# Two expert layers in a two-block transformer: gather operands split in two and stored by column, weight ring turned, first-norm modulation moved

## The chip, the cores and the metric

The kernel runs on one core of a Trainium2 chip. A time is the device time of one execution in microseconds (us). The kernel before took 1819.6, 1820.46 and 1828.07 us in three runs, median 1820.46 us. PE is TensorE, DVE is VectorE, ACT is ScalarE, POOL is GpSimd, and SP is the engine whose queue issues the transfers spoken of here. 1 MB below is 1,048,576 bytes, the size of one weight chunk.

## The reference, cut to what matters

There are 256 tokens of width 1024. The first block has two layers: layer 0 with a convolution and attention mixer, layer 1 with a recurrent one, each followed by a mixture of experts. All values are 32-bit floats.

```python
for layer in range(2):
    mod = silu(c) @ mod_w[layer] + mod_b[layer]
    sh1, sc1, g1, sh2, sc2, g2 = split(mod, 6)
    h = rms_norm(x, mix_norm_g[layer]) * (1 + sc1) + sh1
    mix = even_mixer(h, ...) if layer == 0 else odd_mixer(h, ...)
    x = x + g1 * mix
    h = rms_norm(x, ffn_norm_g[layer]) * (1 + sc2) + sh2
    x = x + g2 * moe(h, ...)          # 16 experts, 2 per token

# in moe, for every expert e with its tokens tok and gates g
xb = h2[tok]                                         # gather
y = (silu(xb @ w1[e]) * (xb @ w3[e])) @ w2[e]        # w1, w3: 1024 x 512, w2: 512 x 1024
out[tok] += y * g
```

The second block has two layers of feed-forward, attention with a gating unit, and feed-forward. The change does not touch it.

## The kernel before, in words

**Experts.** In an expert layer all 16 experts are computed, sorted by how many tokens they have. Seven groups stand in `GROUPS`: the first holds two experts with up to 64 rows each, the others fewer rows and more experts. For each group the weights come in as chunks of 1 MB, four for w1, four for w3, four for w2 (the last group twice as many): 96 chunks a layer. A *unit* is one group (the first) or two; `unit_of` gathers the tokens of a unit: a 0/1 matrix `oh` picks token rows on TensorE. Then per group: `up` with w1 (L1095), `Silu` (L1156), `up` with w3, the product `hm` (L1255), `turn` (four transposes, L1101), `down` with w2 (L1114), gates and `combine` (L1131, L1132), which adds to x. Of a group `down` is done while the next group is in `up`. The weight chunks are the stationary or moving operands without any conversion.

**Gather.** `xn` holds the normalised tokens, 32-bit, [token, tile, 1024]. The gather (L1038) reads a column block of `xn` as stationary operand with every fourth column (`512 * (k // 4) + k % 4 : ... : 4`) and `oh` as 32-bit moving operand. Each such matmul stands as two records in the trace. DVE and ACT copy its result out (L1049, L1052).

**Weights and queue.** SP issues the chunk transfers in program order, and each waits until its buffer's last reader is done. There are ten buffers `raw` of 1 MB in the expert phase, and four pairs `rawwH`/`rawwL` of 0.5 MB each, which share their memory tags with the split weights `wH`/`wL` of the mixers. `chunks` takes the ten and then the four in turn (`turns["all"]`); `load` takes only `raw`. At the start of an expert layer some buffers are still held by the mixer's out projection (the pairs) or by `mod_rows` (four `raw`). A further wait on SP is the load of the order of the experts (`idsi`, L1145), from which the addresses of all chunks after the first expert group's come.

**Split.** `loadw` and `split` (L301, L303) make two rounded parts H and L of a 32-bit weight: ACT writes H = round(w), DVE or POOL writes L = w - H. The mixers' projections are then three passes, H*H, L*H and H*L (L558 to L560).

**Modulation.** `mod_rows(layer, part, row)` makes one part of `mod` along the free axis: 4 MB of `mod_w`, 64 records of L365, an addition on DVE (L402), a broadcast by eight records of L407, two ACT copies (L409). `mod_cols` makes parts along partitions. Both are put into the mixers as `fills`, work for TensorE while it would wait; `FILL1` sets how many go to which place in layer 1.

**Order.** The program is written as a list of operations, and a scheduler then sets the order on each engine. An `If` on a flag (L1198, L1199) ends the expert layer: an overflow path for experts with more rows than their group allows, which is not taken here. Before it stands `ahead_of`, in which the first loads of the next stage are issued; no instruction moves across the `If`.

**Between layers.** Behind the `If` come the norm of x (square sums L448, L450; power -0.5 on POOL L335; `xn` L463, L464), transposes (L475), features `f` (L481, L483), `hH`/`hL` (L605, L606), and the projection of the odd mixer (L558 on).

## Time and profile before

| | us |
|---|---|
| median of three runs | 1820.46 |
| the profiled execution | 1823.28 |
| its span in the trace | 1821.1 |
| mixer of layer 0, to its last matmul | 0 to 201 |
| experts of layer 0 | 201 to 465 |
| norm, features, mixer of layer 1 | 465 to 582 |
| experts of layer 1 | 582 to 836 |
| second block | 842 to 1821 |

The profiled execution took 2.2 us more than its span. Engine shares over the whole span say little here, since the second block takes over half of it and has its own limit. The stages named in the table have to be looked at one by one: for each, whether TensorE waits, or the transfers do, and who releases them.

### The profile page before, as it was taken

Reading aid. Unit: us, or ns where it says so; the run is one execution under the profiler, and the core shown is the slowest. Engines: PE = TensorE matmul, PEld = TensorE weight load, DVE = VectorE, ACT = ScalarE, POOL = GpSimd, SP = SyncE. Lnnn points to the kernel's source line nnn. Section 1 sums busy time; section 2 is a strip of 40 time slices with the busy share of each in tenths; the row PEclk is TensorE's granted clock in tenths of the full one; section 3 lists DMA queues with packets and bytes.
Section 4 is the critical chain, followed back from the end, with each engine's and each line's share of the span. In section 5 each row is a group of like instructions: output and inputs, shape, how many; then the busy total and the mean of one; then the engine's idle time right before and its main releaser. Section 6 shows DMA issues by size and latency. Waiting matters only on the chain.

```text
span 1821.1 us, 23880 instructions
## 1 busy us (share of the span) xinstructions
PE 1735.9 (95%) x9320; PEld 1226.5 (67%) x9320; DVE 901.9 (50%) x1570; ACT 710.2 (39%) x1100; POOL 96.2 (5%) x138
## 2 busy tenths in 40 slices
PE   6899999998798999988999999999999999999998
PEld 4765744432675544335888888888888888888886
DVE  3893533112657522124555564655465546655554
ACT  2434311100464211004444556544354446664443
POOL 0580000000100000000000000000000000000000
PEclk9999999999899999998999999999999999999999
DMA  9947689999986899999655653555555555426530
GB/s 363 347 165 270 240 333 395 373 407 416 348 292 246 311 371 415 418 417 351 226 186 174 198 178 101 185 185 185 185 182 185 182 184 191 158 93 208 184 118 23
DMA packets 148651, 454.80 MB, mean 250 GB/s; under 512 B 8608, under 2 KB 18992, under 8 KB 130608
## 3 DMA queue, kind: packets, MB, share of 16 engines
q1 hardware_dynamic: 148528, 453.16, 67.6%
q8 instruction: 77, 1.26, 0.3%
q14 instruction: 46, 0.38, 0.1%
HBM read 452.07 MB, written 1.05 MB: 249 GB/s over the span
## 4 chain that ended last, share of the span: by engine, by line
PE 52%; ACT 0%; issue 0%; DVE 0%; POOL 0%; DVEq 0%; POOLq 0%; ACTq 0%
PE acc L321 16%; PE acc L323 16%; PE acc L322 16%; PE tp L1281 1%; PE acc L1434 1%; PE tp L491 1%; PE acc L1344 1%; PE tp L1428 0%; PE tp L1398 0%; PE acc L1373 0%; PE acc L1338 0%; ACT t L448 0%; PE acc L1339 0%; PE acc L1340 0%; ACT wH L301 0%
## 5 line engine op out<-in xcount | busy, mean ns | idle before, releaser
L303 DVE TENSOR_TENSOR wL<-raw,wH 128x1024 fp32r<-128x1024 f32 x369 | 452.5, 1231 | 400.2 <-ACT wH L301 399.5
L301 ACT ACTIVATE wH<-raw 128x1024 fp32r<-128x1024 f32 x372 | 391.0, 1058 | 425.9 <-PE acc L323 393.4
L321 PE MATMUL acc<-wH,xTH 128*128 128x512 f32 (+1 forms) x928 | 353.2, 381 | 1.2 <-ACT xTH L494 1.1
L323 PE MATMUL acc<-wH,xTL 128*128 128x512 f32 (+1 forms) x928 | 349.0, 379 | 0.2 <-DVE xTL L495 0.2
L322 PE MATMUL acc<-wL,xTH 128*128 128x512 f32 (+1 forms) x928 | 349.2, 377 | 0.0
L323 PEld LDWEIGHTS acc<-wH,xTL 128*128 128x128 f32 x928 | 174.7, 188 | 35.0 <-DVE xTL L495 1.6
L321 PEld LDWEIGHTS acc<-wH,xTH 128*128 128x128 f32 x928 | 175.1, 189 | 33.5 <-ACT xTH L494 2.1
L322 PEld LDWEIGHTS acc<-wL,xTH 128*128 128x128 f32 x928 | 175.2, 189 | 32.8
L1095 PE MATMUL acc<-raw,xg 128*64 128x512 f32 (+1 forms) x960 | 180.4, 596 | 0.0
L322 PE MATMUL acc<-wL,tH 128*128 128x512 f32 x352 | 139.1, 395 | 0.0
L321 PE MATMUL acc<-wH,tH 128*128 128x512 f32 x352 | 138.1, 392 | 0.0
L323 PE MATMUL acc<-wH,tL 128*128 128x512 f32 x352 | 137.9, 392 | 0.0
L1095 PEld LDWEIGHTS acc<-raw,xg 128*64 128x64 f32 (+1 forms) x960 | 52.1, 123 | 100.4 <-issue 95.9
L1114 PE MATMUL acc<-raw,tf 128*32 128x512 f32 (+1 forms) x416 | 86.3, 598 | 2.9 <-DMA raw<-in_ex_w_dram 2.9
L365 PE MATMUL acc<-raw,condb 128*32 128x256 f32 x768 | 71.5, 491 | 10.6 <-DMA raw<-in_mod_w_dram 10.6
L558 PE MATMUL acc<-hH,wH 128*128 128x256 f32 x256 | 75.9, 297 | 5.7 <-ACT wH L301 5.7
L1255 DVE SCALAR_TENSOR_TENSOR hm<-acc,gg,hm 128x512 f32<-128x512 f32 x14 | 10.5, 751 | 140.6 <-PE acc L1095 96.5
L335 POOL TENSOR_TENSOR rs<-ms,mhalf 128x1 f32<-128x1 f32 x22 | 12.1, 553 | 1252.2 <-DVE ms L334 1238.1
L321 PEld LDWEIGHTS acc<-wH,tH 128*128 128x128 f32 x352 | 66.1, 188 | 14.8
L323 PEld LDWEIGHTS acc<-wH,tL 128*128 128x128 f32 x352 | 66.1, 188 | 14.0
L322 PEld LDWEIGHTS acc<-wL,tH 128*128 128x128 f32 x352 | 66.2, 188 | 13.5
L560 PE MATMUL acc<-hH,wL 128*128 128x256 f32 x256 | 74.3, 293 | 0.5 <-DVE wL L303 0.5
(366 smaller groups left out, 2201.2 us busy)
## 6 DMA issues: line engine op xcount, KB each, us to landing
raw<-in_ex_w_dram SPq DMA_DIRECT2D x140, 1024.0 KB, 11.5
raw<-in_ffn_w_gate_dram SPq DMA_DIRECT2D x44, 1024.0 KB, 5.1
raw<-in_ffn_w_up_dram SPq DMA_DIRECT2D x44, 1024.0 KB, 5.2
raw<-in_ffn_w_down_dram SPq DMA_DIRECT2D x44, 1024.0 KB, 4.9
raw<-in_mod_w_dram SPq DMA_DIRECT2D x64, 512.0 KB, 8.1
rawwH<-in_ex_w_dram SPq DMA_DIRECT2D x52, 512.0 KB, 11.5
rawwL<-in_ex_w_dram SPq DMA_DIRECT2D x52, 512.0 KB, 11.4
raw<-in_w_in_dram SPq DMA_DIRECT2D x20, 1024.0 KB, 5.1
```

The lines of the kernel that those rows point to most:

```text
L301: S.activation(H, src, AF.Copy)
L303: eng.tensor_tensor(L, src, H.bitcast(F32), op=OP.subtract)
L321: TE.matmul(o, aH, bH, start=start, stop=False)
L322: TE.matmul(o, aH, bL, start=False, stop=False)
L323: return TE.matmul(o, aL, bH, start=False, stop=stop)
L365: TE.matmul(ps[32 * i:32 * i + 32, :], condb[:, k, :], quarter(raw[:, k % 2], i), start=k == 0, stop=k == 7)
L491: TE.transpose(ps[:, j, :], src[:, j * P:(j + 1) * P], ident)
L558: TE.matmul(o, ws[kk][0][:, cs], hH[:, k, :], start=k == 0 and c % 2 == 0, stop=False)
L560: TE.matmul(o, ws[kk][1][:, cs], hH[:, k, :], start=False, stop=k == 7 and c % 2 == 1)
L1095: TE.matmul(ps[c:c + w, :], xg[:, k, c:c + w], ws[e][j], start=k == 0, stop=k == 7)
L1114: TE.matmul(y[h][c:c + w, :], tf[:, k, c:c + w], ws[e][j][:, half(h)], start=k == 0, stop=k == 3)
L1281: TE.transpose(ps[:, j, :], hm[:, j * P:(j + 1) * P], ident)
```

## The change

It has six parts. (1) `xn` is replaced by `xH` and `xL`, the two rounded parts, stored [token, tile, column block, 128], so that a column block is contiguous. ACT writes the normalised row permuted into a scratch tile (`t512`, a ring of two that `add_rows` uses as well), ACT makes `xH`, POOL makes `xL`. The gather becomes 32 single-record matmuls where it was 16 of two records. (2) The rows of w2 are taken as `p*4+j`, so that `hm` is stored [row, 4, 128]: `Silu` and the product write with a stride, the transposes read contiguous. (3) `turns["all"]` starts at 3 instead of 0: chunks 1 to 6 go to `raw`, 7 to 10 to the four pairs, then `raw` again. (4) `order_of`, which gives `idsi`, is called ahead of the first gather. (5) Before the `If` of layer 0 the 4 MB of `mod_w` for `mod_rows(1, 2)` are queued (`rows_load`), then 2 MB of `od_in`, whose first split stands ahead of the `If` still. `mod_rows(1, 2)` moves from the middle of the odd mixer to the place right behind the norm (`fills(1)`). (6) `Singly`, which only the overflow path uses, holds one 512-wide tile.

```diff
-FILL1 = (0, 1, 1)
+SOON = (6, 6)
+FILL1 = (0, 1, 0)
...
+    def rows_load(layer, part):
+        for u in range(4):
+            early[layer, part, u] = load(kp(a["mod_w"][layer])[:, 2 * u:2 * u + 2, part * D:(part + 1) * D])
...
-            self.xn = pl.tile([P, 2, D], F32, name="xn", bufs=1)
+            self.xH, self.xL = [pl.tile([P, 2, KD, P], F32R, name=n, bufs=1) for n in ("xH", "xL")]
...
-                    S.activation(self.xn[:, t, half(hh)], x[:, t, half(hh)], AF.Copy, scale=self.r[:, t:t + 1])
+                    xn, ks = small([4, P], "t512"), slice(4 * hh, 4 * hh + 4)
+                    S.activation(xn.rearrange("p k q -> p q k"), x[:, t, half(hh)].rearrange("p (q k) -> p q k", k=4),
+                                 AF.Copy, scale=self.r[:, t:t + 1])
+                    split(self.xH[:, t, ks, :], self.xL[:, t, ks, :], xn, G)
...
             hL = featL = pf.tile([P, KD, T], F32R, name="hL")
+            fills(1)
             input_features(hH, hL, nx, A, B)
...
-                            TE.matmul(ps[:, kk, :], xn[:, t, 512 * (k // 4) + k % 4:512 * (k // 4) + 512:4],
-                                      oh[:, t, :N].bitcast(F32), start=t == 0 and kk == 0, stop=t == 1 and kk == 1)
+                            for part in (xH, xL):
+                                TE.matmul(ps[:, kk, :], part[:, t, k, :], oh[:, t, :N],
+                                          start=part is xH and t == 0 and kk == 0, stop=part is xL and t == 1 and kk == 1)
...
-                    TE.transpose(pt[:, k, :], hm[:, 256 * (k // 2) + k % 2:256 * (k // 2) + 256:2], ident)
+                    TE.transpose(pt[:, k, :], hm[:, k, :], ident)
...
-                hm = px.tile([P, 512], F32, name="hm")
-                S.activation(hm, h1, AF.Silu)
+                hm = px.tile([P, 4, P], F32, name="hm")
+                S.activation(by_row(hm), rows_in(h1), AF.Silu)
...
-            turns.pop("all", None)
+            turns["all"] = sum(n for _, n in raws) - SOON[layer] - 1
             for kind in range(3):
                 for hf in range(2):
                     weights(0, kind)(hf, True)
+            first = one_hot((0,), pos)
+            order_of()
+            weights(1, 0)(0, True)
+            gates_of()
             unit_of(0)
             in_order()
-            weights(1, 0)(0, True)
...
                 def ahead_of():
 
+                    if not layer:
+                        rows_load(1, 2)
                     for hf in range(2):
-                        unit(*((first_ffn, 0) if layer else (od_in, D)), hf, False, lead=() if layer else LEAD[hf])
+                        unit(*((first_ffn, 0) if layer else (od_in, D)), hf, False if layer else "raw")
```

On SP at the start of the experts of layer 0, before (a row `raw` is a 1 MB chunk, a pair `rawwH`, `rawwL` is one chunk too; `idsi` is the order of the experts):

```order
L266 DMA raw<-in_ex_w_dram 128x2048 x10
L279 DMA rawwH<-in_ex_w_dram 128x1024
L279 DMA rawwL<-in_ex_w_dram 128x1024
L279 DMA rawwH<-in_ex_w_dram 128x1024
L279 DMA rawwL<-in_ex_w_dram 128x1024
L1145 TENSOR_LOAD idsi
```

and of the changed kernel at the same place:

```order
L267 DMA raw<-in_ex_w_dram 128x2048 x6
L280 DMA rawwH<-in_ex_w_dram 128x1024
...
L280 DMA rawwL<-in_ex_w_dram 128x1024
L267 DMA raw<-in_ex_w_dram 128x2048 x2
L1166 TENSOR_LOAD idsi
```

The dots stand for six rows, the rest of four pairs. Chunks 7 to 10 moved from `raw` to the pairs, chunks 11 and 12 from the pairs to `raw`; the wait for `idsi` stands behind chunk 12 in both.

On ACT around the `If` at the end of the experts of layer 0, before (`yp` is the last group's result, `raw_3358` and `raw_3368` the first two chunks of `od_in`, `t512` a scratch tile for the square sums):

```order
L301 ACTIVATE yp_3332<-yg_3338 128x512
L301 ACTIVATE wH_3360<-raw_3358 128x1024
L301 ACTIVATE wH_3364<-raw_3358 128x1024
L1198 TENSOR_LOAD flagi_1765
...
L448 ACTIVATE t512_4370,ss4_4368<-x_75 128x512
L301 ACTIVATE wH_3370<-raw_3368 128x1024
L301 ACTIVATE wH_3374<-raw_3368 128x1024
L448 ACTIVATE t512_4372,ss4_4368<-x_75 128x512
L448 ACTIVATE t512_4379,ss4_4368<-x_75 128x512
L464 ACTIVATE xn_4442<-x_75,rs_4369 128x512 x2
L481 ACTIVATE f_4447<-tp_4448,A11_4389 128x256
```

and of the changed kernel (`raw_3447` and `raw_3449` are the first two chunks of `od_in`, queued behind 4 MB of `mod_w`):

```order
L303 ACTIVATE yp_3413<-yg_3419 128x512
L303 ACTIVATE wH_4748<-raw_3447 128x1024
L303 ACTIVATE wH_4752<-raw_3447 128x1024
L1226 TENSOR_LOAD flagi_1778
...
L457 ACTIVATE t512_4571,ss4_4569<-x_75 128x512
L457 ACTIVATE t512_4573,ss4_4569<-x_75 128x512
L457 ACTIVATE t512_4580,ss4_4569<-x_75 128x512
L303 ACTIVATE wH_4804<-raw_3449 128x1024
L476 ACTIVATE xn_4686<-x_75,rs_4570 128x512 x2
L303 ACTIVATE wH_4808<-raw_3449 128x1024
L493 ACTIVATE f_4691<-tp_4692,A11_4590 128x256
```

The first split still stands ahead of the `If`, but its chunk is now the fifth in the queue and not the first; half of the second split stands between the `xn` and the first `f`.

On PE behind the same `If`, of the changed kernel (before, one row of 16 transposes L475 stood between the `If` and L558; L573 is what L558 was):

```order
L1227 UNCONDITIONAL_BRANCH
L367 MATMUL acc<-raw,condb 32x256 x32
L487 MATMUL tp<-cst,xn 128x128 x8
L416 MATMUL acc<-t_4640,cst 128x256 x4
L487 MATMUL tp<-cst,xn 128x128 x8
L573 MATMUL acc<-hH,wH 128x256
```

The matmuls of `mod_rows(1, 2)` (L367) and its broadcast (L416) moved here, the broadcast between the two halves of the transposes; each such matmul stands as two records in the trace.

## Rows read from the trace of the kernel before

**Rows 1.** The page, part 1: busy time, share of the span, instructions.

```profile
PE 1735.9 (95%) x9320; PEld 1226.5 (67%) x9320; DVE 901.9 (50%) x1570; ACT 710.2 (39%) x1100; POOL 96.2 (5%) x138
```

**Rows 2.** Windows, experts of layer 0: stretch, length, busy per engine, PEclk, DMA share, GB/s.

```profile
195.00:210.00 15.00, 12.88 (x96) 9.34 (x98) 8.93 (x28) 5.44 (x11) 2.05 (x20) 0.84 0.07 29
...
253.00:280.00 27.00, 27.00 (x179) 7.96 (x171) 4.02 (x6) 2.46 (x4) 0.00 (x0) 1.00 0.71 254
...
355.00:360.00 5.00, 5.00 (x20) 2.01 (x20) 0.83 (x3) 0.00 (x0) 0.00 (x0) 1.00 0.29 61
360.00:459.00 99.00, 91.77 (x442) 31.83 (x444) 19.23 (x34) 8.05 (x15) 0.00 (x0) 1.00 1.01 410
```

**Rows 3.** Windows, experts of layer 1, same columns.

```profile
643.00:660.00 17.00, 17.00 (x116) 6.39 (x116) 5.39 (x9) 1.90 (x4) 0.00 (x0) 1.00 0.86 298
660.00:831.00 171.00, 161.34 (x814) 65.53 (x809) 35.94 (x64) 17.11 (x32) 0.00 (x0) 0.99 1.02 416
```

**Rows 4.** Waits of SP's queue, 185 to 480 us: total, times, longest.

```profile
SPq L266 <- PE acc L1095: 71.6, 33, 15.5
...
SPq L266 <- PE acc L365: 20.3, 4, 18.2
```

**Rows 5.** Timeline of SP's issues: start, time, engine, line, transfer.

```profile
210.46 3.71 SPq L266 DMA_DIRECT2D raw<-in_ex_w_dram  x4
...
224.94 0.36 SPq L279 DMA_DIRECT2D rawwH<-in_ex_w_dram  x1
...
230.18 28.40 SPq L266 DMA_DIRECT2D raw<-in_ex_w_dram  x10
```

**Rows 6.** Windows, records of L1038 alone (busy PE, PEld, PEclk, DMA share, GB/s).

```profile
217.00:228.00 11.00, 8.19 (x32) 7.69 (x32) 1.00 1.02 403
241.00:251.00 10.00, 7.82 (x32) 7.54 (x32) 1.00 1.01 419
```

**Rows 7.** Groups by line on PE: busy us, mean ns of one | idle before.

```profile
L1281 PE MATMUL tp<-cst,hm 128*128 128x128 f32 x176 | 23.9, 273 | 0.0
```

**Rows 8.** Groups by line on PEld, same columns.

```profile
L1038 PEld LDWEIGHTS tp<-oh,xn 128*128 128x128 f32 x256 | 61.9, 327 | 14.5 <-issue 10.0 <-ACT xg L1049 4.4
...
L1281 PEld LDWEIGHTS tp<-cst,hm 128*128 128x128 f32 x176 | 20.4, 141 | 3.7 <-DVE tL L303 1.0
```

**Rows 9.** Timeline of PE between the layers.

```profile
473.57 2.33 PE L475 MATMUL tp<-cst,xn 128*128 128x128 f32 x8 [9.11 <-DVE xn L463]
...
477.96 0.44 PE L558 MATMUL acc<-hH,wH 128*128 128x256 f32 x1
478.24 0.28 PE L559 MATMUL acc<-hL,wH 128*128 128x256 f32 x1
478.36 0.28 PE L560 MATMUL acc<-hH,wL 128*128 128x256 f32 x1
```

**Rows 10.** Groups by line on POOL, same columns.

```profile
L699 POOL TENSOR_TENSOR cv<-cv,tap 128x256 f32<-128x256 f32 x30 | 29.2, 973 | 0.1
...
L303 POOL TENSOR_TENSOR wL<-raw,wH 128x1024 fp32r<-128x1024 f32 x3 | 7.0, 2356 | 256.1 <-ACT wH L301 256.1
```

**Rows 11.** Timeline of ACT, end of the mixer of layer 0.

```profile
198.72 1.34 ACT L457 ACTIVATE xn<-x,rs 128x512 f32<-128x512 f32 x2 [0.37 <-POOL rs L335]
```

**Rows 12.** Timeline of DVE there: the last addition to x.

```profile
202.20 1.28 DVE L502 TENSOR_TENSOR x<-x,t 128x512 f32<-128x512 f32 x2
```

**Rows 13.** Timeline of ACT between the layers.

```profile
462.42 1.99 ACT L301 ACTIVATE wH<-raw 128x1024 fp32r<-128x1024 f32 x2
466.00 0.63 ACT L448 ACTIVATE t<-x 128x512 f32<-128x512 f32 x1 [1.59 <-DVEq L1199]
```

**Rows 14.** Records of L365 in the odd mixer: count, times, first and last start.

```profile
L365 PE MATMUL acc<-raw,condb x64: 379/379/403, 501.2 to 504.5; 128*32 128x256 f32 x64
```

**Rows 15.** Timeline of PE in the odd mixer: the broadcast.

```profile
506.31 1.99 PE L407 MATMUL acc<-t,cst 128*128 128x256 f32 x8 [1.41 <-DVE t L402]
```

**Rows 16.** Timeline of PE at the end of the experts of layer 0.

```profile
457.50 0.62 PE L1114 MATMUL acc<-rawwH,tf 128*32 128x512 f32 x1 [0.67 <-DMA rawwH<-in_ex_w_dram]
```

More of the change, by code (lines that the diff above doesn't have):

```diff
@@ L283, with __init__, __getitem__ @@
     class Singly:
-        def __init__(self, ap, pl):
-            self.ap, self.pl, self.held = ap, pl, {}
-        def __getitem__(self, j):
-            if j not in self.held:
-                v = self.pl.tile([P, 1024], F32, name="one", bufs=2)[:, :self.ap.shape[2]]
-                nc.sync.dma_start(v, self.ap[:, j, :])
-                self.held[j] = v
-            return self.held[j]
+        def __init__(self, ap, pl, j=None):
+            self.ap, self.pl, self.j = ap, pl, j
+        def __getitem__(self, at):
+            if self.j is None and self.ap.shape[2] > 512:
+                return type(self)(self.ap, self.pl, at)
+            j, cols_ = (at, slice(0, 512)) if self.j is None else (self.j, at[1])
+            v = self.pl.tile([P, 512], F32, name="one", bufs=1)
+            nc.sync.dma_start(v, self.ap[:, j, cols_])
+            return v
     def after(ins):
@@ L305, with loadw @@
     turn_of = [0]
-    def loadw(ap, pool_every=0, lead=(), begin=None, then=None):
-        w = load(ap)
+    def loadw(ap, pool_every=0, lead=(), begin=None, then=None, w=None):
+        w = load(ap) if w is None else w
         n, b = ap.shape[1] // 2, ap.shape[2]
@@ L399, in mod_rows, with get @@
         w = kp(a["mod_w"][layer])[:, :, part * D:(part + 1) * D]
-        ps = mod_quarters([once(lambda u=u: load(w[:, 2 * u:2 * u + 2, :])) for u in range(4)],
+        def get(u):
+            return lambda: early.pop((layer, part, u), None) or load(w[:, 2 * u:2 * u + 2, :])
+        ps = mod_quarters([once(get(u)) for u in range(4)],
                           lambda raw, i: raw[:, 256 * i:256 * i + 256])
@@ L535, in out_proj @@
                 take(t, h)
-    ahead = {}
+    ahead, fetched = {}, {}
     def unit(wi, col, u, take=True, **kw):
-        if not take:
-            ahead[id(wi), col, u] = loadw(wi[:, 4 * u:4 * u + 4, col:col + 512], **kw)
+        key, ap = (id(wi), col, u), wi[:, 4 * u:4 * u + 4, col:col + 512]
+        if take == "raw":
+            fetched[key] = load(ap)
+        elif not take:
+            ahead[key] = loadw(ap, **kw)
         else:
-            return ahead.pop((id(wi), col, u), None) or loadw(wi[:, 4 * u:4 * u + 4, col:col + 512], **kw)
+            return ahead.pop(key, None) or loadw(ap, w=fetched.pop(key, None), **kw)
     def proj_f(wi, col, hH, hL, lead=((), ()), then=None, ps=None, halves=(0, 1)):
@@ L1004, in in_order @@
                 V.scalar_tensor_tensor(one, at(rk), 1.0, down_(slot), op0=OP.add, op1=OP.is_equal)
-                def picked(o, v):
-                    V.tensor_mul(tmp, one, at(v))
-                    V.tensor_reduce(o[:, :NS], tmp, axis=AX.X, op=OP.add)
-                    if v is not slot:
-                        V.tensor_copy(o[:, NS:], v[:, NS:16])
                 picked(ids16, slot)
@@ L1015, in in_order @@
                 V.tensor_copy(idsi[:, :16], ids16)
+            def in_order():
                 for t in range(2):
@@ L1254, in moe @@
                 hm = hm_
[L1255 removed]
+                times(hm, h3, gg)
                 if n % 2 == 0 and n < n_groups - 1:
```

43 lines of the change are left out of this document (26 added, 17 removed).

## The prediction

> **What bounds the kernel now.** I read the page first, then windows of busy time and transfer rate by stage, then the waits of SP's queue, and the timelines where one stage ends and the next begins. TensorE is busy for 95% of the span [rows 1], but that is a mean over stages with two limits. The second block, over half of the span, is not changed. In the two expert layers the transfers are the limit: from 360 to 459 us the DMA share is 1.01 at 410 GB/s while TensorE idles 7.2 us of 99, and from 660 to 831 us it is 1.02 at 416 GB/s with 9.7 us idle [rows 2, 3]. One chunk (1,048,576 bytes) at 416 GB/s is 2.52 us. TensorE's last wait for a weight in layer 0 ends at 457.50 [rows 16]; half a chunk, 1.26 us, is still to come, so the expert weights have landed at about 458.8. I call that moment X. A saving on TensorE inside an expert layer counts only as far as it moves X, that is, as far as buffers come free earlier at a place where the transfers stood still. Such places, against 416 GB/s: 195 to 210 us loses 14.0 us (29 GB/s), 253 to 280 loses 10.5 (254 GB/s), 355 to 360 loses 4.3 (61 GB/s), 360 to 459 loses 1.4 [rows 2]. In layer 1 the stretch from 643 to 660 loses 4.8 [rows 3].
>
> **Gather.** The 32 records of the first gather keep TensorE busy 8.19 us, those of a later one 7.82 [rows 6]. Each stationary load takes 327 ns, against 141 ns for one read in contiguous columns [rows 8]. The new form has 32 matmuls of one record. At 256 columns the rounded form starts every 0.12 us (478.24, 478.36) [rows 9]: 32 x 0.12 = 3.8 us. At 128 columns the nearest row has 23.9 us for 176, 0.136 us each [rows 7], so 4.3 us at most. The saving is 8.2 - 4.1 for the first unit and 7.8 - 3.8 for the three others: 16 us of TensorE per layer, 32 in all. If the rounded form were no faster than the old records (0.24 us each), the saving is zero; if all of it were on the path, 32 us. I take neither, since TensorE waits for weights at the end.
>
> **What of it moves X.** The early turn of the ring lets chunks 7 to 10 start at about 197 instead of 210.46 [rows 5], since the out projection frees the pairs sooner than `mod_rows` frees four `raw` (SP waits 18.2 us for it in one stretch) [rows 4]. That fills some 10 us of the first hole. But SP issues in order, and the pairs then hold the first half of w2 of the first group, so that the two chunks behind number 22 wait for `down` of that group, where before they waited for `up` of the next (15.5 us, the longest wait) [rows 4]. By the gathers TensorE is about 6 us earlier there, by a later start of the router (below) 2 us later, and the pair is read later in the program: chunk 24 comes within 1 us of the old time, so the early start is lost again behind it. What remains are the holes behind chunk 24: 4.2 of the 10.5 us (the rest is that wait), 4.3 at 355 to 360, which is the gather of two units holding up `up`, and 1.4: together 9.9 us. TensorE is then 6 to 10 us ahead, which closes such holes. Layer 0: -10, with ends -13 (chunk 24 a little early too) and -3 (new stalls). In layer 1 the hole is 4.8 us, of which I take off 2 us for the later router: -2.8, ends -5 and +1. At the end of the layer the last chunk is a whole `raw` instead of two halves, so TensorE starts it half a chunk later: +1.3 in layer 1; in layer 0 the next stage waits for transfers anyway.
>
> **Router.** `xL` is made by POOL. From 0.973 us at 256 elements and 2.356 at 1024 [rows 10], 512 elements are 1.43 us by interpolation. ACT begins the normalised row at 198.72 with 0.7 us for each half [rows 11]; with two `xH` of about 0.6 the POOL subtractions run to about 203.6. They hold both scratch tiles that the last additions to x need, which before ended at 203.48 [rows 12]. The last addition ends at about 205.6: +2.1 us for everything up to the first gather, in both layers. It is hidden in layer 0 and charged above in layer 1. The earlier order of the experts gives back at most 1.8 us on SP, at 224.94 [rows 5]. The strided writes of `xn` and `hm` I cost at nothing: `Silu` and the product stand beside `up`; without that cover they would cost some tenths of a microsecond per group.
>
> The rows show that a strided read costs a load 327 instead of 141 ns [rows 8]. The Trainium skill, SBUF — State Buffer, section "Door 1: The DMA port swizzle", says that accesses which go to a new 16-byte line each time pay a penalty. By that rule the new writes of the row, 512 bytes apart, would be slower; with the ratio of these loads, 2.3, four of 0.7 us become 1.6 each, and the sum would be about 3.6 us worse in layer 1. The same page's section "Who interferes with whom" has a DVE instruction with two inputs from SBUF block a POOL instruction that reads; no row here separates that from POOL's own time.
>
> **Between the layers.** The first split of `od_in` stays ahead of the `If`, but its chunk now lands behind four of `mod_w`: X + 5 x 2.52 = X + 12.6. Before, ACT ran the two halves at 462.42 to 464.41 and began the square sums at 466.00, X + 7.2 [rows 13]. Now the halves end at X + 14.6, the square sums begin at X + 16.2, and POOL's second `wL` (2.36 us) [rows 10] stands ahead of the power, which gives `xn` at X + 19.5. Then DVE has the next `wL` and the addition of `mod_rows` ahead of `f`, and the eight broadcast records (2 us) stand between the transposes. The projection starts at X + 28; before it started at 477.96 [rows 9], X + 19.2: +8.8 us. The 64 records of `mod_rows` fall in the time in which TensorE waits for `mod_w` anyway. What goes from the odd mixer is 3.66 us of L365 (501.2 to 504.9) [rows 14], 1.41 of waiting and 1.99 of broadcast [rows 15]: -7.1. Net +1.7. Ends: -6 if the scheduler's order costs nothing, +9 if the odd mixer had slack for those 7.1 us.
>
> **Sum.** -10 - 2.8 + 1.3 + 1.7 = -9.8 us. Against the profiled execution, 1823.28, that is 1813.5. That execution is 2.8 us above the median of the runs, 1820.46, to which I hold the forecast: 1810.7.
>
> **Rivals.**
> - Forecast, 42%: 1803 to 1817.
> - More comes out, 17%: chunk 24 comes 3 us earlier, all holes close, and the late start between the layers costs only what `mod_rows` saved: -13 - 5 + 1.3 - 3 = -20, 1801 us. For it: TensorE is ahead by 6 us when those chunks are wanted. Against it: the pair is the last of the group to be read.
> - Nothing, 23%: the holes move instead of closing, since SP's order and the eight chunks under way set them. Then -2.5 in layer 0 and 0 in layer 1, with +1.3 and +1.7: 1821. For it: 71.6 us of SP's waiting is on `up` [rows 4], which is not shorter.
> - Slower, 13%: ACT stands at the first split of `od_in` with four chunks ahead of it, and the odd mixer had room for `mod_rows`, so that the 8.8 us stay. This decides from the point where layer 0 gains under 5 us: -3 + 8.8 + 1.3 + 2 = +9, 1829.5. For it: the order of ACT is fixed ahead of the `If`. Against: TensorE waited only 9.11 us there and is busy behind it.
> - By the rule on lines, 5%: strided writes make ACT late in each router phase: -9.8 + 3.6 and as much for the groups' `hm`, 1818.
>
> **How the numbers follow.** Half a per cent is 9.1 us, about what a measurement tells from no change: faster is below 1811.4. The forecast lies just inside it, and of its own range the part below that bound is the larger one by the holes that could close, so of its 42% I count 28 as faster and 14 as the same; more, 17, is faster; "nothing" gives 21 to the same and 2 to slower, the rule 5 to the same, "slower" 13 to slower. That is faster 0.45, same 0.40, slower 0.15. The range 1798 to 1828 takes in the full closing of the holes at one end and most of the slow case at the other; the likeliest case by itself is 1803 to 1817.
>
> **What would show it.** Right: the gather's records fall to about 4 us per unit; SP issues chunks 7 to 10 near 197 and waits for `down` behind chunk 22; the dip at 355 to 360 is gone; the projection starts some 28 us behind X, and L367 stands ahead of the transposes; the odd mixer is 7 us shorter. Wrong: the last weight of layer 0 lands at 456 or later, or TensorE waits for rows of the gather, or the second block's time changes.

## The result, and the profile after

The change makes the kernel slower: 1834.23 us median (1832.84 to 1836.38) against 1820.13 (1819.6 to 1828.07) for the kernel before, four runs each, a ratio of 1.0068 with the interval 1.0039 to 1.0098. The forecast was 1810.7 with a range of 1798 to 1828; the time lies above it. The profiled execution has a span of 1834.6 us where the one before had 1821.1, and a mean granted clock of 0.973 where it had 0.982.

I read the two traces stage by stage, each stage from one instruction that both kernels have to the next (us from the span's start):

| where | before | after | the stage alone | predicted for it |
|---|---|---|---|---|
| first gather, layer 0 | 217.8 | 219.5 | +1.7 | +2.1 |
| last combining matmul, layer 0 | 464.1 | 462.7 | -3.1 | -12 |
| first matmul of the odd mixer's projection | 478.0 | 485.0 | +8.4 | +8.8 |
| first matmul of its recurrent gates | 527.1 | 527.5 | -6.6 | -7.1 |
| first addition to x | 575.9 | 580.2 | +3.9 | 0 |
| first gather, layer 1 | 595.5 | 604.6 | +4.8 | +2 |
| last combining matmul, layer 1 | 836.1 | 851.2 | +6.0 | -3.5 |
| last matmul | 1813.6 | 1826.5 | -2.2 | 0 |

The predicted end of layer 0's experts was -10 in all, and the 3.5 of layer 1 are the 4.8 us of its hole taken whole, less 1.3 for the last chunk. So the two moves between the layers, the largest changes in the table, were sized well, and they nearly cancel. The loss is in layer 1 and its approach, and layer 0's experts gave 3 us where 12 were expected.

The page's first part, beside [rows 1]:

```profile
PE 1724.8 (94%) x9320; PEld 1201.3 (65%) x9320; DVE 908.8 (50%) x1570; ACT 722.0 (39%) x1108; POOL 106.6 (6%) x146
```

TensorE has less to do, ACT and POOL more. Now the windows of layer 0, which answer to [rows 2] (length, busy time of PE, PEld, DVE, ACT and POOL, granted clock, DMA share, GB/s):

```profile
195.00:210.00 15.00, 10.96 (x77) 8.11 (x75) 7.51 (x20) 7.24 (x12) 4.57 (x22) 0.82 0.78 291
...
220.00:225.00 5.00, 3.79 (x24) 3.53 (x24) 4.83 (x22) 0.91 (x2) 0.00 (x0) 0.66 0.00 0
225.00:230.00 5.00, 5.00 (x18) 2.91 (x20) 5.00 (x35) 2.58 (x4) 0.00 (x0) 0.50 0.88 331
230.00:235.00 5.00, 5.00 (x20) 1.46 (x18) 4.52 (x31) 0.00 (x0) 0.00 (x0) 0.82 0.36 116
...
253.00:280.00 27.00, 26.96 (x179) 7.38 (x172) 3.79 (x5) 2.76 (x4) 0.00 (x0) 1.00 0.59 221
355.00:360.00 5.00, 5.00 (x25) 1.85 (x26) 0.93 (x6) 0.41 (x1) 0.00 (x0) 1.00 1.01 421
360.00:459.00 99.00, 86.08 (x397) 28.37 (x394) 18.72 (x27) 7.02 (x11) 0.00 (x0) 0.97 1.02 416
```

The dip at 355 us is gone (421 GB/s where there were 61), and the early start is there (291 against 29). But 220 to 225 us moves nothing at all, and the hole from 253 to 280 us, of which 4.2 us were to close, grew instead: 221 GB/s against 254. Layer 1 begins 9.1 us later than before, so its windows are counted from the first gather (604.6 and 595.5): 20 us from 30 us behind it on, then the next 20. First after, with the long stretch that answers to [rows 3] as a third line, then before:

```profile
634.60:654.60 20.00, 20.00 (x158) 6.33 (x159) 3.57 (x14) 3.21 (x6) 0.00 (x0) 1.00 0.38 137
654.60:674.60 20.00, 20.00 (x152) 9.46 (x152) 6.33 (x13) 3.24 (x5) 0.00 (x0) 1.00 0.97 380
657.00:843.00 186.00, 169.99 (x876) 61.73 (x875) 41.40 (x70) 21.06 (x35) 0.00 (x0) 0.97 1.01 415
```

```profile
625.50:645.50 20.00, 20.00 (x161) 8.25 (x161) 3.66 (x15) 3.17 (x7) 0.00 (x0) 1.00 0.71 274
645.50:665.50 20.00, 20.00 (x156) 7.23 (x156) 5.15 (x8) 2.46 (x4) 0.00 (x0) 1.00 0.89 328
```

The hole costs 20 x (274 - 137) / 416 = 6.6 us of transfer time more than before, and the next 20 us give 20 x (380 - 328) / 416 = 2.5 back. The first 5 us behind the gather lose another 4.8 (nothing moves, where before had 397 GB/s), and the 22 us ahead of the gather gain 2.1 by the early start (280 GB/s against 240). That is 6.8 us, near the 6.0 by which the stage is longer. Behind it the transfers are saturated (1.01), so nothing more comes back.

Who holds the queue is in the waits of SP, 185 to 480 us, which answer to [rows 4]:

```profile
...
SPq L267 <- PE acc L1116: 28.7, 15, 7.5
SPq L280 <- PE acc L1135: 21.1, 2, 15.1
...
SPq L1166 <- DVE pos L1018: 9.9, 1, 9.9
```

L280 issues the pairs, L1135 is `down`. Two waits of the pairs for `down` take 21.1 us, and one of them, 15.1 us, is now the longest wait. The timeline of SP's issues shows where they stand, first in layer 0, then in layer 1:

```profile
243.96 0.33 SPq L280 DMA_DIRECT2D rawwH<-in_ex_w_dram  x1
244.58 0.33 SPq L280 DMA_DIRECT2D rawwL<-in_ex_w_dram  x1
260.56 0.34 SPq L280 DMA_DIRECT2D rawwH<-in_ex_w_dram  x1
267.13 0.33 SPq L280 DMA_DIRECT2D rawwL<-in_ex_w_dram  x1
...
629.96 0.33 SPq L280 DMA_DIRECT2D rawwL<-in_ex_w_dram  x1
651.91 0.34 SPq L280 DMA_DIRECT2D rawwH<-in_ex_w_dram  x1
653.63 0.33 SPq L280 DMA_DIRECT2D rawwL<-in_ex_w_dram  x1
```

Chunk 22 goes out at 243.96 and 629.4, then the queue stands, until chunk 23 follows at 260.56 with its first half. In the kernel before the queue stands behind chunk 22 too, but for `up`, and is let go earlier. These are its chunks 23 and 24 in either layer:

```profile
257.30 1.28 SPq L266 DMA_DIRECT2D raw<-in_ex_w_dram  x2
...
635.68 0.91 SPq L266 DMA_DIRECT2D raw<-in_ex_w_dram  x2
```

Two pairs, chunks 25 and 26, go out right behind them (258.80 to 260.45 and 636.80 to 638.53), and only then does the queue stand at `down` of the first group. So that stop came four chunks earlier in the queue by the change: chunk 23 is 3 us late with its first half in layer 0 and 10 with its second, 16 and 18 in layer 1, of which 9.1 are the later start of the layer.

Why the second half comes 6.6 us behind the first in layer 0 is in the timeline of PE:

```profile
257.51 1.06 PE L1116 MATMUL acc<-raw,xg 128*32 128x512 f32 x6
258.60 1.93 PE L1135 MATMUL acc<-rawwH,tf 128*64 128x512 f32 x6
260.46 3.62 PE L1116 MATMUL acc<-raw,xg 128*32 128x512 f32 x26
264.01 0.64 PE L1135 MATMUL acc<-rawwH,tf 128*64 128x512 f32 x1
264.02 0.64 PE L1135 MATMUL acc<-rawwL,tf 128*64 128x512 f32 x1
...
266.01 1.50 PE L1135 MATMUL acc<-rawwL,tf 128*64 128x512 f32 x5
```

`down` of the first group (L1135) does not run through: it begins on `rawwH` at 258.60, `up` of the next group (L1116) stands between, and `rawwL` is read to the end only at 267.5. One wait for a pair is a wait for the whole interleaved stretch.

The gather's records by themselves, in the windows of [rows 6] (PE, PEld, granted clock, DMA share, GB/s):

```profile
217.00:228.00 11.00, 6.04 (x32) 5.51 (x32) 0.71 0.36 133
241.00:251.00 10.00, 4.26 (x32) 3.88 (x32) 1.00 1.00 409
```

At the full clock the 32 records take 4.26 us where they took 7.82, and a stationary load takes 205 to 207 ns where it took 327 [rows 8]. The first gather keeps TensorE for 6.04 us since the granted clock falls to 0.50 in that place; before it was 1.00 there.

### The profile page after: what moved, and what is told of

It is laid out like the page before. It is cut to its first block, busy times and chain, and to the rows that moved or that the text cites. A ratio compares the mean times of both kernels' runs of the same rounds, so it can differ in the third digit from the quotient of the medians.

```text
span 1834.6 us, 23902 instructions
## 1 busy us (share of the span) xinstructions
PE 1724.8 (94%) x9320; PEld 1201.3 (65%) x9320; DVE 908.8 (50%) x1570; ACT 722.0 (39%) x1108; POOL 106.6 (6%) x146
## 4 chain that ended last, share of the span: by engine, by line
PE 52%; DVE 0%; issue 0%; ACT 0%; POOL 0%; DVEq 0%; POOLq 0%; ACTq 0%
PE acc L323 16%; PE acc L325 16%; PE acc L324 16%; PE tp L1313 1%; PE acc L1466 1%; PE tp L503 1%; PE acc L1376 1%; PE tp L1460 0%; DVE wL L305 0%; PE tp L1430 0%; PE acc L1405 0%; PE acc L1370 0%; PE acc L1371 0%; PE acc L1372 0%; ACT wT L1462 0%
## 5 line engine op out<-in xcount | busy, mean ns | idle before, releaser
L1116 PE MATMUL acc<-raw,xg 128*32 128x512 f32 (+1 forms) x896 | 174.9, 633 | 11.5 <-DMA raw<-in_ex_w_dram 11.2
L1116 PEld LDWEIGHTS acc<-raw,xg 128*32 128x32 f32 (+1 forms) x896 | 46.8, 126 | 118.7 <-issue 87.6
L1135 PE MATMUL acc<-raw,tf 128*32 128x512 f32 (+1 forms) x512 | 111.3, 598 | 4.9 <-DMA raw<-in_ex_w_dram 4.9
L1185 DVE SCALAR_TENSOR_TENSOR hm<-acc,gg,hm 128x512 f32<-128x512 f32 x14 | 15.6, 1112 | 182.8 <-PE acc L1116 126.1
L303 ACT ACTIVATE yp<-yg 128x512 fp32r<-128x512 f32 x28 | 17.6, 628 | 208.8 <-DVE yg L1144 208.8
L367 PE MATMUL acc<-raw,condb 128*32 128x256 f32 x768 | 73.8, 504 | 20.1 <-ACTq L1227 9.6
L573 PE MATMUL acc<-hH,wH 128*128 128x256 f32 x256 | 76.0, 298 | 5.7 <-ACT wH L303 5.7
```

Source lines behind the costliest of these rows:

```text
L303: S.activation(H, src, AF.Copy)
L367: TE.matmul(ps[32 * i:32 * i + 32, :], condb[:, k, :], quarter(raw[:, k % 2], i), start=k == 0, stop=k == 7)
L573: TE.matmul(o, ws[kk][0][:, cs], hH[:, k, :], start=k == 0 and c % 2 == 0, stop=False)
L1116: TE.matmul(ps[c:c + w, :], xg[:, k, c:c + w], ws[e][j], start=k == 0, stop=k == 7)
L1135: TE.matmul(y[h][c:c + w, :], tf[:, k, c:c + w], ws[e][j][:, half(h)], start=k == 0, stop=k == 3)
```

## The experiments

All are changes of the kernel after, unless said. In the expectations A is the theory that the ring's new turn costs the time (A1: by what the pairs then hold), C2 that the early order of the experts does, D that the place of the column filler does, T that the place of `od_in` does. The others are told in words. The kernel before was measured again beside each set of runs, with medians of 1820.1 to 1822.1 us, so a difference of medians between two changed kernels is uncertain by one or two microseconds; the ratio to before, which stands behind each time, is the better measure.

**The ring's turn undone.**

```
-            turns["all"] = sum(n for _, n in raws) - SOON[layer] - 1
+            turns.pop("all", None)
```

> The changed kernel with one part undone: the ring of weight buffers starts at 0 again (chunks 1 to 10 raw, 11 and 12 pairs), all else as changed. Theory A (the turned ring makes the two chunks behind number 22 wait until down of the first group has read its pairs): chunks 23 and 24 are released by up again, the hole of the transfers at 253 to 270 us shrinks by 6 us, that at 640 to 655 by about 10, and the time falls by 12 to 18 us, to 1816 to 1822. Theory B (TensorE comes late out of the router and runs at half clock, whatever the ring): the time stays within 4 us of the changed kernel's 1834.

1826.25 us, 1.0021 (1.0009 to 1.0034) of before: 8 us of the 14 come back, less than expected. The experts of layer 1, from the first gather to the last combining matmul, take 238.1 us; after has 246.6 and before 240.6. In layer 0 it is 240.9 against 243.2 and 246.3. The windows of the first hole:

```profile
253.00:280.00 27.00, 26.93 (x174) 7.64 (x169) 5.45 (x18) 4.00 (x7) 0.00 (x0) 1.00 0.69 259
```

259 GB/s is close to the old 254. So the rest of the change does shorten the experts by 5.4 and 2.5 us, and the turn takes 2.3 and 8.5 of it away.

**The turn alone, put into the kernel before.**

```
-            turns.pop("all", None)
+            turns["all"] = 3
```

> The kernel before with one part added: the ring starts at 3 in both layers. Theory A (chunks 23 and 24 wait for down of the first group, which costs more than the early start of chunks 7 to 10 gives): 6 to 11 us slower than before, most of it in layer 1. Rival (the turn hurts only where the router is late): within 3 us of before.

1833.17 us, 1.0069 (1.0052 to 1.0086): the one line costs as much as the whole change. Two windows, of this kernel and then of before:

```profile
253.00:265.00 12.00, 12.00 (x80) 3.43 (x72) 0.00 (x0) 1.19 (x2) 0.00 (x0) 1.00 0.17 49
628.00:642.00 14.00, 14.00 (x124) 4.34 (x116) 0.75 (x1) 1.19 (x2) 0.00 (x0) 1.00 0.01 3
```

```profile
253.00:265.00 12.00, 12.00 (x92) 3.44 (x84) 0.00 (x0) 1.19 (x2) 0.00 (x0) 1.00 0.62 228
628.00:642.00 14.00, 14.00 (x130) 4.80 (x133) 2.36 (x13) 2.32 (x5) 0.00 (x0) 1.00 0.59 229
```

In layer 1 the transfers stand still for 14 us (3 GB/s). The experts there take 249.1 us against 240.6. In layer 0 the early start pays for the stall (246.1 against 246.3). The longest wait of a pair for `down` in layer 1 is 20.3 us; before it was 9.5. The traced execution is 7.7 us longer than the traced one of before, and layer 1's experts alone are 8.5 longer; where the rest of the 12.5 us between the medians goes, no trace shows.

**The turn kept, with other chunks in the pairs.**

```
-SOON = (6, 6)
+SOON = (4, 4)
```

> The changed kernel with SOON = (4, 4): the ring is turned further, so that chunks 5 to 8 (w3 of the first group) go to the pairs and chunks 9 to 16 to raw. The pairs are wanted again by chunks 19 to 22. Theory A1 (what costs is that the pairs hold the first half of w2, which down of the first group reads late): SP no longer waits for down ahead of chunk 23, the hole at 253 to 268 us shrinks to what the kernel before has, and the time is 1820 to 1827, as with the ring from 0 or better. Rival A2 (any turn from 0 costs, by the order of the rest of the ring): 1832 or more.

1823.41 us, 1.0013 (1.0003 to 1.0022), 10.8 us below after. The pairs now hold chunks 5 to 8, the four of w3, whose reader `up` comes one step earlier in the program than `down`. The window and the issues of this kernel:

```profile
253.00:265.00 12.00, 11.93 (x90) 3.35 (x84) 0.00 (x0) 1.51 (x2) 0.00 (x0) 1.00 0.97 382
```

```profile
247.04 0.34 SPq L280 DMA_DIRECT2D rawwL<-in_ex_w_dram  x1
253.77 21.46 SPq L267 DMA_DIRECT2D raw<-in_ex_w_dram  x10
```

The pause after the pairs is 6.4 us where it was 16, and the experts of layer 0 take 234.8 us, 11.4 less than before the change. That is about the 12 us which the forecast gave this stage, though it looked for them in the holes behind chunk 24 and counted the early start as lost; the gain needs the pairs to hold something that is read soon. In layer 1 the same turn gives 242.3, still worse than no turn (238.1): SP still waits once for `down` there, now with a `raw` (7.4 us). So what the pairs hold is about half of the turn's cost in layer 1; the rest stays with the turn itself.

**The first split of `od_in` loaded ahead of `mod_w` again**, with `mod_rows` where the change put it.

```
+    for hf in range(2):
+        unit(*((first_ffn, 0) if layer else (od_in, D)), hf, False, lead=() if layer else LEAD[hf])
     if not layer:
         rows_load(1, 2)
-    for hf in range(2):
-        unit(*((first_ffn, 0) if layer else (od_in, D)), hf, False if layer else "raw")
```

> The changed kernel with the two chunks of od_in queued and split ahead of the 4 MB of mod_w between the layers. Theory T (ACT waits at the first split of od_in for the fifth chunk in the queue, which puts the projection of layer 1 at 22 us behind the last expert matmul instead of 13.5): the projection starts 5 to 7 us earlier, and the time is 1827 to 1830. Rival: TensorE then waits for mod_w, which now lands last and stands ahead of the transposes, and the scan of the odd mixer sets its end anyway: the time is 1832 to 1836.

1828.1 us, 1.0032 (1.0015 to 1.0048): 6.1 us less than after. Timelines of ACT and of PE, after's two first and then this kernel's:

```profile
470.63 2.00 ACT L303 ACTIVATE wH<-raw 128x1024 fp32r<-128x1024 f32 x2 [9.37 <-DMA raw<-in_od_in_w_dram]
472.89 0.63 ACT L457 ACTIVATE t<-x 128x512 f32<-128x512 f32 x1 [0.26 <-ACTq L1227]
```

```profile
472.73 6.04 PE L367 MATMUL acc<-raw,condb 128*32 128x256 f32 x64 [9.60 <-ACTq L1227]
...
485.00 0.36 PE L573 MATMUL acc<-hH,wH 128*128 128x256 f32 x1
```

```profile
461.04 3.88 ACT L303 ACTIVATE wH<-raw 128x1024 fp32r<-128x1024 f32 x4
468.08 0.63 ACT L457 ACTIVATE t<-x 128x512 f32<-128x512 f32 x1 [3.15 <-DVEq L1227]
```

```profile
480.62 0.36 PE L573 MATMUL acc<-hH,wH 128*128 128x256 f32 x1
```

ACT stood 9.37 us for `od_in` behind 4 MB of `mod_w`, and TensorE waited 9.60 for ACT at the `If`. With `od_in` first the square sums (L457) start 4.8 us earlier and the projection 4.4.

**The additions to x without a scratch tile.**

```
-        V.tensor_mul(tmp, ps, row[:, half(h)])
-        V.tensor_add(x[:, t, half(h)], x[:, t, half(h)], tmp)
+        V.tensor_mul(ps, ps, row[:, half(h)])
+        V.tensor_add(x[:, t, half(h)], x[:, t, half(h)], ps)
```

> The changed kernel with the gated addition behind the mixers (add_rows) written through PSUM in place, so that it needs no scratch tile and doesn't wait for POOL's xL. Theory B1 (the shared scratch ring costs the router 2 us a layer): the last addition to x ends 2 us earlier in both layers, first gathers 2 us earlier, and the time falls by 3 to 5 us, to 1829 to 1831. Rival: another wait takes its place (the square sums use the same scratch ring): within 1.5 us of 1834.

1831.91 us, 1.0049 (1.003 to 1.0067): 2.3 us, under what was expected, and by the intervals not clear of after. The trace shows it: the first gathers come 1.7 and 3.3 us earlier. DVE in layer 0, after and then this kernel:

```profile
202.19 0.69 DVE L513 TENSOR_TENSOR t<-acc,g 128x512 f32<-128x512 f32 x1 [4.68 <-POOL xL L305]
...
204.04 1.28 DVE L514 TENSOR_TENSOR x<-x,t 128x512 f32<-128x512 f32 x2
```

```profile
201.95 1.28 DVE L513 TENSOR_TENSOR x<-x,acc 128x512 f32<-128x512 f32 x2
```

The 4.68 us wait for POOL's `xL` is the scratch tile that the prediction named; without it the last addition is back at 201.95 (before: 202.20 [rows 12]).

**The order of the experts worked out late again** (`order_of` behind `unit_of(0)`, the load of the next w1 after it).

```
-            order_of()
-            weights(1, 0)(0, True)
             gates_of()
             unit_of(0)
+            order_of()
             in_order()
+            weights(1, 0)(0, True)
```

> The changed kernel with the order of experts worked out behind the first gather again. Theory C2 (the early order puts DVE's work ahead of the copies out of the first gather, TensorE waits 1.2 us there, its clock falls to half at 222 us): no such wait, the granted clock at 220 to 230 is 0.9 or more, up of the first group ends 3 to 4 us earlier in both layers, and the time falls by 3 to 7 us, to 1827 to 1831. Rival (the rounded gather is too light by itself, or the idle time in the router decides): the clock falls all the same, chunks 13 and 14 come 1.7 us later, and the time is 1834 to 1837.

1834.62 us, 1.0073 (1.0054 to 1.0091): no difference from after. The first gather still waits 1.2 us for ACT, and the clock still falls in it. The theory that the early order is to blame fell.

**The first gather issued twice.** The 32 matmuls of the first unit run once more into the same bank.

```
+    if N == P:
+        for kk in range(2):
+            k = 2 * k2 + kk
+            for t in range(2):
+                for part in (xH, xL):
+                    TE.matmul(ps[:, kk, :], part[:, t, k, :], oh[:, t, :N], ...)
```

> The changed kernel with the first gather's matmuls of each layer issued twice into the same place (the second pass overwrites the first), so TensorE has 3.6 us more to do there. Theory C (the short gather leaves TensorE waiting for the copies out, its granted clock falls to half at 222 us and up runs at half speed until 232): the clock stays at 1.0 there, up is 3 to 5 us shorter, and the time is within 2 us of 1834 although work was added. Rival (the clock has nothing to do with it): up begins 3.6 us later in each layer and the time is 1839 to 1842.

1847.77 us, 1.0137 (1.0113 to 1.0162): 13.5 us more. More work for TensorE in that place did not keep the clock up; it only made the stretch longer, in both layers (from the first gather to the last combining matmul 250.6 us in layer 0 and 250.9 in layer 1).

**The second column filler.**

```
-FILL1 = (0, 1, 0)
+FILL1 = (0, 1, 1)
```

> The changed kernel with FILL1 = (0, 1, 1) as before: one filler of modulation columns goes back behind the first output branch of the odd mixer. Theory D (the moved filler lets the last output branch end late, so that its gelu and with it hH come late to the out projection: stalls of 3.5 and 1.6 us and a fall of the clock at 555 to 566 us): out projection of layer 1 ends 4 us earlier, time 1829 to 1831. Rival: the filler only stands elsewhere and the scan is late anyway: within 1.5 us of 1834.

1839.43 us, 1.0097 (1.0075 to 1.012): slower, against the expectation. The edit was not like for like: since `mod_rows` is already taken from the list of fillers, the second filler now comes ahead of the recurrent gates, which start 11 us later (538.4 against 527.5; 3.5 of them stand already at the projection). From there to the first addition it is 48.9 us, as before the change (48.8); after has 52.7. But the stretch holds no column filler now (7.5 us of TensorE), where both other kernels have one in it, so this run decides nothing on theory D.

**Only the gather and w2's new rows** (ring, early order, fillers and the moves between the layers undone; the edits are those above and these):

```
-FILL1 = (0, 1, 0)
+FILL1 = (0, 1, 1)
...
-            fills(1)
...
-                    if not layer:
-                        rows_load(1, 2)
```

> Of the change only the gather in two rounded parts by column block (with POOL's xL and the rows of w2 as p*4+j); the ring starts at 0, the order of experts is late, and the modulation between the layers is as before. Theory G (TensorE's saving of 32 us is worth nothing because the expert layers wait for transfers, and the router loses 2 us a layer and the clock): 1820 to 1826, no faster than before. Rival (the gather saves, and the other parts spoil it): 1808 to 1815.

1819.0 us, 0.9988 (0.9975 to 1.0001): some 2 us below before, hardly to be told from it, and in neither expected range. The experts take 240.7 and 237.0 us (before 246.3 and 240.6), 9 us less; the stretch from the first addition to the first gather of layer 1 takes back 4.9 (24.5 against 19.6).

**The same with the additions in place of the scratch tile.**

```
...
-        V.tensor_add(x[:, t, half(h)], x[:, t, half(h)], tmp)
+        V.tensor_add(x[:, t, half(h)], x[:, t, half(h)], ps)
```

> Of the change only the gather, with the gated addition in PSUM: no turned ring, order of experts late, between the layers as before. If the router's wait for POOL is what is left of the gather's cost: 2 to 4 us under the run with the gather alone, 0.3 to 0.4% under the kernel before. If the wait is replaced by another: the same as the gather alone, 0.1 to 0.2% under it.

1817.64 us, 0.9978 (0.9969 to 0.9987): faster than before, by 2 to 6 us. Against the run with the gather alone it is 1.4 us by the medians and 1.8 by the ratios, between the two expectations and not clear of noise.

**Three repairs together**: ring undone, `od_in` first, additions without scratch.

```
+            turns.pop("all", None)
...
+                    for hf in range(2):
+                        unit(..., hf, False, lead=() if layer else LEAD[hf])
...
+        V.tensor_add(x[:, t, half(h)], x[:, t, half(h)], ps)
```

> The changed kernel with three repairs: ring from 0, the gated addition in PSUM, od_in ahead of mod_w. If their effects add (ring -8 and addition -2.3 by the runs so far, od_in -5): 1818 to 1820. If the holes only move: 1823 to 1827.

1816.5 us, 0.9968 (0.9955 to 0.9981). Singly they gave 8.0, 6.1 and 2.3 us, 16.4 together; after less 16.4 is 1817.8. They add.

**The three repairs with the old gather** (`xn` in f32, read with a stride, two records each), w2's rows as in the change.

```
-                            for part in (xH, xL):
-                                TE.matmul(ps[:, kk, :], part[:, t, k, :], oh[:, t, :N], ...)
+                            TE.matmul(ps[:, kk, :], xn[:, t, 512 * (k // 4) + k % 4:512 * (k // 4) + 512:4],
+                                      oh[:, t, :N].bitcast(F32), ...)
```

> The kernel with the three repairs, but the old gather: normalised rows in 32 bits, strided columns, two records for each matmul, nothing on POOL. Theory G2 (the new gather moves the end of the expert layers by 4 to 6 us each, as the stretch from the first gather to the last combine says: 240 and 237 us where it was 246 and 241): 4 to 8 us slower than the run with three repairs. Theory C3 (the clock, which falls to half in the first gather in each run with the new one and did not before, takes it back): the granted clock at 215 to 230 stays at 1.0, and the time is within 2 us of the run with three repairs.

1819.37 us, 0.9991 (0.9981 to 1.0). Against the three repairs the medians differ by 2.9 us and the ratios by 0.0023, which is 4.2: so much is the new gather worth here, though a later unit saves 3.6 us of TensorE and the first 2.2. The two intervals touch, so the size is rough. The clock, of this kernel and then of the last kernel below, whose first gather starts within 1 us of this one's:

```profile
215.00:220.00 5.00, 4.80 (x21) 4.53 (x22) 2.76 (x14) 0.46 (x1) 0.00 (x0) 0.66 0.99 416
220.00:225.00 5.00, 5.00 (x20) 4.01 (x20) 2.96 (x12) 0.92 (x2) 0.00 (x0) 1.00 1.02 412
```

```profile
215.00:220.00 5.00, 3.54 (x24) 3.21 (x24) 4.83 (x22) 0.91 (x2) 0.00 (x0) 0.83 0.16 66
220.00:225.00 5.00, 5.00 (x18) 2.92 (x20) 5.00 (x35) 2.58 (x4) 0.00 (x0) 0.50 0.90 329
```

With the old gather TensorE is busy 4.80 of 5 us at the start of the gather, at a mean granted clock of 0.66, and is back at the full clock behind it. With the new one it is busy 3.54 of 5 at 0.83, and the next 5 us run at the half. So the clock falls in both, but for longer with the new gather: as (1 - granted clock) x length these ten microseconds lose 1.7 and 3.4 us. The other traces agree. In or right behind the first gather of layer 0 the kernel before loses nothing, the turn alone 1.7 us, and each run with the new gather 3.4 to 5.1; in layer 1 the three kernels with the old gather lose 1.7 each, those with the new one 3.4 to 5.1. Theory C3 did not come out as it stands: the clock did not stay at 1.0 here, and the time is 2.9 us over the three repairs and not within 2. But part of what the new gather saves does go back into the clock.

**The three repairs and the column fillers in the order 0, 0, 1.**

```
-FILL1 = (0, 1, 0)
+FILL1 = (0, 0, 1)
```

> The kernel with the three repairs (ring from 0, addition in PSUM, od_in first) and FILL1 = (0, 0, 1), by which the last filler of modulation columns stands behind the whole last branch of the odd mixer again and not ahead of its last eight steps. Theory D2 (those last eight steps end 8 us later, so gelu, hH and the out projection come 3 to 4 us late; from the first recurrent-gate matmul to the first addition to x it is 52.5 us where it was 48.8): that stretch falls to 49, the time is 2 to 4 us under the run with three repairs. Rival: the filler only stands elsewhere, same time within 1 us.

1815.41 us, 0.9962 (0.9948 to 0.9975). From the recurrent gates to the first addition it is 50.3 us where the three repairs have 52.5; the total can't be told from theirs. The wait that goes is in the traces: with the order 0, 1, 0 the last filler begins 15.8 us behind the first gate matmul, ahead of the end of the output branch, and the out projection then waits for ACT's `hH` (3.48 us in after, 3.47 in the three repairs). Here and in the kernel before it begins 18.6 us behind it, and that wait is gone.

**The turn with SOON = (4, 4), `od_in` first, additions without scratch, fillers 0, 0, 1.**

```
-SOON = (6, 6)
+SOON = (4, 4)
-FILL1 = (0, 1, 0)
+FILL1 = (0, 0, 1)
...
+        V.tensor_add(x[:, t, half(h)], x[:, t, half(h)], ps)
...
```

> All repairs (addition in PSUM, od_in first, FILL1 = (0, 0, 1)) with SOON = (4, 4) in the place of the ring from 0. If the early start of four chunks is kept without the wait for down: 1 to 5 us under the run with the ring from 0 and the same repairs, 1810 to 1814. If the transfers close their holes alike from 275 us on: the same within 1.5 us. If theory A1 is wrong: 8 us or more over it.

1812.18 us, 0.9958 (0.9944 to 0.9972): the lowest median here, faster than both kernels, by 5 to 10 us against the one before. Against the run above, which has the ring from 0 and the same repairs (0.9962), the ratios tell no difference, so the first two expectations stay undecided. Its experts take 234.5 us in layer 0 and 243.3 in layer 1: the turn gains 6 in the first and loses 6 in the second against the kernels without it. A turn in layer 0 alone was not run.

## Why the prediction was wrong

**The step that failed** is "chunk 24 comes within 1 us of the old time", and with it the sum's -10 and -2.8. It named the right mechanism: the pairs hold the first half of w2, and what is queued behind number 22 then waits for `down` of that group, where it waited for `up`. But it let a TensorE that is 4 us ahead make up for the later place of that read in the program, and TensorE was not ahead: `down` begins at 258.60 in layer 0, where it began at 258.85. In layer 0 `down` is interleaved with the next `up`, so that chunk 24 went out at 267.67 instead of 258.3, 9 us late. Layer 1 I never worked out by itself; there `down` begins at 649.95 instead of 643.25, and chunk 24 goes out at 654.17 instead of 636.3, 18 us late. Counted from the first gather of its layer, chunk 24 is 7.8 us late in layer 0 and 8.8 in layer 1, so the step is the same in both. Behind both places the transfers are saturated, so a late chunk moves the end. The runs show it: the turn alone costs 12.5 us in the kernel before (9.5 to 15.7 by the interval); undone, it gives 8 back; with chunks in the pairs that are read one step earlier, 10.8. The prediction had also named a sign of being wrong, the last weight of layer 0 at 456 us or later, and it came. TensorE's last wait for a weight, now for a whole chunk, ends at 456.25:

```profile
456.25 0.62 PE L1135 MATMUL acc<-raw,tf 128*32 128x512 f32 x1 [0.59 <-DMA raw<-in_ex_w_dram]
```

So X moved from about 458.8 to 456.25, by 2.5 us where 10 were forecast.

**TensorE 6 to 10 us ahead** was wrong too. The gather's records did fall to 0.13 us each at the full clock (predicted 0.12 to 0.136), and the dip at 355 us closed. But the first gather starts 1.7 us later, and then the clock falls to 0.50 inside it. By the windows the three stretches of 5 us from 220 to 235 lose (1 - 0.66) x 5 + (1 - 0.50) x 5 + (1 - 0.82) x 5 = 5.1 us by that, where before had 1.00 throughout, so that at 258.6 us TensorE is where it was. In all, the gather is worth 3 to 4 us of the total, where 16 us of TensorE per layer were to open the way for 10 and 3.

**The early start** came as said (chunks 7 to 10 from 195.78). Part of it was lost at once: from 220 to 225 us nothing moves, since SP waits 9.9 us for the order of the experts, where it had waited 7.2. The early order of the experts gave nothing, as the run with the late one shows.

**Router.** +2.1 us in layer 0 was +1.7. POOL's subtraction was interpolated at 1.43 us and takes 1.29. In layer 1 it was taken as +2, and it is 4.8: 2.4 within the additions and 2.4 behind them. The first part goes with the scratch tile. In the second the strided writes have a share, which I had costed at nothing. Groups of ACT by form, after and then before:

```profile
L1178 ACT ACTIVATE hm<-acc 128x512 f32<-128x512 f32 x14 | 15.0, 1071 | 119.9 <-PE acc L1116 119.9
...
L467 ACT ACTIVATE t<-x,rs 128x512 f32<-128x512 f32 x8 | 8.6, 1179 | 2.7 <-POOL rs L337 2.7
```

```profile
L1156 ACT ACTIVATE hm<-acc 128x512 f32<-128x512 f32 x14 | 8.4, 597 | 93.2 <-PE acc L1095 93.2
...
L457 ACT ACTIVATE xn<-x,rs 128x512 f32<-128x512 f32 x8 | 5.3, 716 | 3.7 <-POOL rs L335 3.7
```

The normalised row takes 1179 ns a half instead of 716, `Silu` 1071 instead of 597, and the product on DVE 1112 instead of 751. These are 1.5 to 1.8 times the old ones. The Trainium skill, SBUF — State Buffer, section "Door 1: The DMA port swizzle", has accesses that go to a new 16-byte line each time pay a penalty. The rows agree in direction, and the estimate by the ratio of the loads, 2.3, was too high. With four halves it is 1.9 us of ACT per router, where I estimated 3.6. Little of it reaches the path: from the first addition to the first gather of layer 1 the run with the old gather, which has neither these row writes nor `xL`, takes 22.2 us, the three repairs 22.8 and the kernel before 19.6. What the changed kernels share there is the clock, granted 0.86 in after (580 to 604 us) and 0.84 with the old gather (572 to 594), where before had 1.00 (575 to 595); that it makes the rest is not shown. That rule had 5% as a rival; it was right on the operation and small in the sum.

**Between the layers** the steps held one by one: +8.4 for +8.8, -6.6 for -7.1, net +1.8 for +1.7. ACT stands at the first split, as the rival on the slower side had it, but its other half, that the odd mixer had room for `mod_rows`, did not come: the mixer is shorter by what left it. That rival had the right sign for a reason that is only part of the loss; even with `od_in` first the kernel stays slower than before.

**What I left out** are the 3.9 us from the recurrent gates to the first addition, which I had at 0 without a reason. The new `FILL1` leaves one column filler in that stretch, as before, but lets it begin 2.8 us earlier, and `hH` then comes late; with the order 0, 0, 1 that wait is gone and 2.2 us of the stretch with it. The rest is open: with the fillers of before the same stretch takes 50.4 us in the run with the gather and the additions in PSUM, and the last kernel has 48.8 with the fillers that gave 50.3 above.

Open are also the cause of the longer fall of the clock at the first gather (it stays in all runs with the new gather, also with the gather doubled, with the late order and with an earlier start), the share of w2's new rows, which no run takes out by itself, and the 2.2 us that the second block is shorter.

## What to carry to other kernels

When a ring of buffers is turned, write down for each buffer which reader frees it and at what time the last of its reads ends, not when the first starts, and do it for every stage that uses the ring: an in-order queue stands at the latest of them. Here two turns of one ring differ by 10.8 us by which chunks lay in four of fourteen buffers. A saving on an engine that waits for transfers counts for what it lets start earlier, so price a change there by the bytes that move in each window, and take every rearranged write at its own price on the engine that makes it.

## What the runs showed of the hardware

- TensorE's clock was granted at 1.2 GHz (0.50) for longer at the first gather once that gather was lighter: (1 - granted clock) x length is 3.4 to 5.1 us in each expert layer of each run with the new gather, and 0 or 1.7 with the old one. Why, the runs don't tell.
- A write of 512 f32 elements per partition with a stride of 512 bytes takes ACT and DVE 1.5 to 1.8 times as long (1071 against 597 ns, 1179 against 716, and 1112 against 751 for DVE's product, which reads `hm` with the same stride too).
- A stationary load of 128 x 128 takes 205 ns from contiguous rounded columns and 327 from f32 ones with a stride.
